# Opening stage of a two-layer trunk: two products instead of three, weights ahead of the modulation units, 256 channels at a time

## The chip, the cores and the metric

The kernel runs on one core of a Trainium2 chip. The metric is the device time of one execution in microseconds (us). The engines of the core are TensorE (PE, with PEld for its weight loads), VectorE (DVE), ScalarE (ACT), GpSimd (POOL) and SyncE (SP), whose queue issues nearly all transfers here. Sixteen DMA engines move the data.

## The reference

A decoder trunk of two layers over 256 tokens and 2048 channels, in float32. What matters here is how layer 0 begins:

```python
shift, scale, gate = jnp.split(jax.nn.silu(c) @ ada_w + ada_b, 3, axis=-1)
h = x * (1.0 + scale) + shift
proj = h @ w_in                      # q, k, v, o, gates of mLSTM | r, k, v, low ranks of RWKV-7
ya = _mlstm(...)                     # chunked matrix memory, 8 heads of 128
yb = _rwkv7(...)                     # state of 64 x 64 for 16 heads
y = jnp.concatenate([ya, yb], -1) @ w_out
x = layer_norm(ALPHA * x + (1.0 + gate) * y, ...)
```

After it follow a SwiGLU sub-layer and a second layer (retention and gated DeltaNet, then SwiGLU), each with a modulation of its own. The change leaves them as they are.

## The kernel before

**Products.** A product is h (256 tokens x 2048 channels) times 512 columns of weights. Float32 operands are split into two parts of type fp32r: ScalarE rounds a weight tile to `hi` (line 693), VectorE subtracts to get `lo` (line 694), and three matmuls per 128 channels and 128 tokens are summed in PSUM (lines 708 to 710: h's high part times `hi`, times `lo`, h's low part times `hi`). A *unit* is the part of a product over 512 channels (a quarter of the 2048): one weight tile of 128 x 2048 (1024 KB, from `w_ab`), two `hi` and two `lo` tiles of 128 x 1024, and 24 matmuls (2 halves x 2 token tiles x 2 blocks of 128 channels x 3). The weight tiles come in through a ring of three buffers, `raw`; the `hi` and `lo` tiles have three buffers each. A product has two banks of PSUM, out of a pool "g" of three; there are pools "m" of three and "c" of two beside it.

**Modulation (adaLN) units.** The vector silu(c) @ ada_w is 192 columns of 128 values. Each column is one unit: a weight tile of 128 x 2048 (1024 KB, `ada`) is multiplied on VectorE by `silu_c`, which holds silu(c) in all 128 partitions, and summed along the row (line 634, a SCALAR_TENSOR_TENSOR and a small read of the accumulator). After 8 units (4 shifts, 4 scales) lines 642 to 645 make bias and scale of 4 x 128 channels.

**Opening stage** (`setup`, `first_products`, `first_h`). It loads the constants (`cols`, `cons`, `crow` broadcast to 128 partitions, `rows`), applies Silu, and goes through the four quarters of the channels. For each quarter: 8 modulation units, then h for 512 channels (line 770 on ScalarE, 757 and 758 on VectorE), then a unit of each of four products: the low ranks (304 columns, `w_low`) and blocks 0, 1 and 2 of RWKV's columns. All eight PSUM banks are taken by these four products. Even modulation units use the ring `raw`, odd ones a larger pool `a`; all the weights of the products use `raw`. So 32 modulation units of 1024 KB and 16 weight tiles go in.

**Behind it** (`mixer_ab`, `rwkv`). RWKV runs in four batches of four heads; each has a front part and a chain of small float32 matmuls and VectorE steps (an inverse among them). The other products of layer 0 (RWKV blocks 3 to 5, mLSTM blocks 6 to 9, then 10 to 13) come in program order behind the batches: two after batch 0, two after batch 1, three after batch 2, the last four in the second mLSTM group. Results wait in two tiles `zt`, or go to DRAM (`put_by`). After each unit of a product, `fill(rate)` adds modulation units at 48/44 per unit: 48 of them over the 44 units of the 11 products.

**Order.** At the end of the program a planner (`Plan`) lists all instructions and fixes an order for every engine: lower program order first among what is ready, with the splits of a product moved 2000 places ahead. An instruction that opens a tile must wait until the ring of that tile has a free buffer, in program order within the ring. On the chip each engine, and SP's queue, then runs in this fixed order.

Lines that the steps below name: 597 to 611 (constants), 630 and 671 (transfers of weights), 634 (modulation), 642 to 645 (bias and scale), 693 and 694 (split), 708 to 710 (matmuls), 757, 758 and 770 (h), 1074 and 1082 (results out of PSUM), 998 to 1031 and 1188 to 1264 (RWKV's chain), 1322 (mLSTM's convolution).

Of the kernel before, what the change touches and what calls it, by code (L numbers as in the profile page):

```python
# [21 lines left out]
P = 128  # L22
# [13 lines left out]
LEVELS = (16, 32, 64)  # L36
HEAD = ("qz", "aa", "ss")
# [488 lines left out]
class Trunk:  # L526
# [67 lines left out]
    def setup(self):  # L594
        nc, fix = self.nc, self.fix
        self.cols = fix.tile([P, NCOLS], F32, name="cols_sb")
        nc.sync.dma_start(self.cols[:], self.ins["cols"])
        self.cons = fix.tile([P, NCONS], F32, name="cons_sb")
        nc.sync.dma_start(self.cons[:], self.ins["cons"])
        self.ident = self.con("ident")  # L600
        self.sc = fix.tile([P, D], F32, name="silu_c")
        nc.sync.dma_start(self.sc[:], self.ins["crow"].to_broadcast([P, D]))
        nc.scalar.activation(self.sc[:], self.sc[:], AF.Silu)
        o = COLS["mu_r"][0]
        self.keep = fix.tile([P, 27], F32, name="one_less_mu")
# [5 lines left out]
        nc.sync.dma_start(self.rows[:], self.ins["rows"].to_broadcast([P, 32]))  # L611
# [12 lines left out]
    def ada_unit(self, u, deep):  # L624
# [10 lines left out]
        ob = COLS["adab"][0] + 48 * sub  # L635
        if i < 32:
# [7 lines left out]
            if sub == 0:  # L644
                v.tensor_copy(bi, sh)
            else:
                og, ol = COLS["lng"][0] + 16 * (sub - 1) + 4 * g, COLS["lnb"][0] + 16 * (sub - 1) + 4 * g
                v.tensor_tensor(bi, self.cols[:, ol:ol + 4], sc, ALU.mult)
                v.tensor_tensor(bi, bi, sh, ALU.add)
                v.tensor_tensor(sc, self.cols[:, og:og + 4], sc, ALU.mult)  # L650
# [18 lines left out]
    def raw(self, src):  # L669
        w = self.raw_p.tile([P, 2048], F32, tag="raw", name=self.name("raw"))  # L670
# [3 lines left out]
    def split(self, src, n, ahead=2000, homes="ss"):  # L674
# [3 lines left out]
        with self.tc.high_priority(offset=ahead):  # L678
            w = self.raw(src)
# [80 lines left out]
    def first_h(self, g):  # L760
        nc = self.nc
        act = self.h_p.tile([P, 2, 4, T], F32R, tag="h", name=self.name("h"))
        for k2 in range(2):
            h32 = self.t2([P, 2, T])
            x = self.t2([P, 2, T])
            o = (4 * g + 2 * k2) * T
            nc.sync.dma_start(x[:], self.ins["xt"][:, o:o + 2 * T].rearrange("p (k t) -> p k t", k=2))
            for j in range(2):
                k = 4 * g + 2 * k2 + j
                nc.scalar.activation(h32[:, j, :], x[:, j, :], AF.Identity, bias=self.ab[:, 0, 16 + k:17 + k], scale=self.ab[:, 0, k:k + 1])  # L770
            self.into(act, slice(0, T), h32[:], slice(2 * k2, 2 * k2 + 2))
        return act
# [319 lines left out]
    def rwkv_tiles(self, zt, block):  # L1092

        nc = self.nc
        if block == 5:
            src, zt = zt, self.own([P, NT, 512], "zt", 2)
            self.fetch(zt, src)
# [169 lines left out]
    def first_products(self):  # L1267

        w, low = self.ins["w_ab"], self.ins["w_low"]
        srcs = [[low[i] for i in range(KG)]] + [[w[4 * b + i] for i in range(KG)] for b in range(3)]  # L1270
        banks = [[self.bank(k) for k in kinds] for kinds in ("gg", "gm", "mm", "cc")]
        h = []
        for g in range(KG):
# [5 lines left out]
        return h, [banks[0], self.by_tokens(banks[1])] + [self.by_tokens(banks[2 + i], two[:, i]) for i in range(2)]  # L1279

    def rwkv(self, product, early, beside, after):
# [6 lines left out]
        made = 0  # L1288
        last = None
        for i in range(4):  # L1290
# [17 lines left out]
            if i == 0:  # L1308
                tokens += [self.by_tokens(product(3 + j)) for j in range(2)]
            elif i == 1:  # L1310
                tokens.append(self.put_by(product(5)))
            after(i)
# [372 lines left out]
    def mixer_ab(self, h, rate, early):  # L1685
# [7 lines left out]
        def spilled(i, out):  # L1693
# [3 lines left out]
            if i == 2:  # L1697
# [3 lines left out]
        def direct(i, out):  # L1701
            banks = product(10 + i)
# [9 lines left out]
        def after(i):  # L1712
            for _ in range((0, 1, 3, 0)[i]):
# [58 lines left out]
def body(tc, ins, out):  # L1772
    with ExitStack() as stack:
# [6 lines left out]
        side = k.mixer_ab(h, 48.0 / 44, early)  # L1780
# [28 lines left out]
```

## Time and profile before

| | us |
|---|---|
| median of 3 runs (2826.0 to 2829.94) | 2829.93 |
| the profiled execution | 2830.83 |
| its span, first to last instruction | 2829.1 |
| PE busy (95%) | 2684.7 |
| DVE busy (72%) | 2023.7 |
| ACT busy (45%) | 1260.0 |

The mean granted clock of TensorE was 0.977 of full speed. DMA moved 683.80 MB, 242 GB/s over the span. Matmuls are pipelined, so that neighbours overlap in their busy times; the pitch from start to start is what they cost. Where a row gives a granted clock, 1.00 is 2.4 GHz and 0.50 is 1.2 GHz; what lies between is a mean over both.

### The profile page before, as it was taken

To read this page: it belongs to the slowest core of one execution; us is meant where nothing else is said; L and a number is where in the kernel's file an instruction comes from. 1 tells how busy PE (TensorE), PEld (TensorE's weight loads), DVE (VectorE), ACT (ScalarE), POOL (GpSimd) and SP (SyncE) were. 2 spreads that over 40 slices of the span, in tenths; PEclk is the share of its full clock that TensorE was granted. 3 is DMA by queue.
4 is the path that set the end of the run, shared out by engine and by line. 5 is a ranking of instruction groups with operands and counts; after the bars stand their busy time and mean duration, and the time that the engine had idled before them with its cause. 6 is when DMAs were issued, how large, how long until landed. Compare 5 with 4: busy or idle time off the path is not lost.

```text
span 2829.1 us, 33250 instructions
## 1 busy us (share of the span) xinstructions
PE 2684.7 (95%) x12622; PEld 2204.3 (78%) x12622; DVE 2023.7 (72%) x3189; ACT 1260.0 (45%) x1670; POOL 72.0 (3%) x88
## 2 busy tenths in 40 slices
PE   3699999899999999999999999999999999999997
PEld 2577777687788787888778888888778888888886
DVE  7889777677867557767767898885876646557557
ACT  1364443537544444443346544344454444443442
POOL 0000000100000000000000111000000000000000
PEclk9899998799999999999999999999999999999999
DMA  9878565255568668877865776675656757666554
GB/s 401 328 268 300 182 233 213 76 194 206 206 233 324 252 237 320 323 273 289 307 254 191 260 281 213 234 256 197 223 208 250 261 189 262 226 213 239 190 191 164
DMA packets 110536, 683.80 MB, mean 242 GB/s; under 512 B 12516, under 2 KB 15784, under 8 KB 32168
## 3 DMA queue, kind: packets, MB, share of 16 engines
q1 hardware_dynamic: 108936, 679.05, 65.8%
q10 hardware_dynamic: 1440, 2.62, 0.2%
q8 instruction: 99, 1.62, 0.2%
q14 instruction: 61, 0.50, 0.0%
HBM read 670.58 MB, written 11.04 MB: 241 GB/s over the span
## 4 chain that ended last, share of the span: by engine, by line
PE 64%; DVE 9%; DMA 8%; ACT 2%; issue 1%; POOL 0%; DVEq 0%; ACTq 0%
PE g L709 19%; PE g L710 19%; PE g L708 19%; DMA raw<-gu 3%; DVE lo L694 3%; DMA raw<-ada 2%; DVE raw L634 2%; ACT hi L693 1%; PE m L1017 1%; PE m L1024 1%; DMA t<-x 1%; DMA raw<-w_cd 1%; PE m L952 1%; DMA raw<-dn 1%; PE m L1031 0%
## 5 line engine op out<-in xcount | busy, mean ns | idle before, releaser
L694 DVE TENSOR_TENSOR lo<-raw,hi 128x1024 fp32r<-128x1024 f32 (+3 forms) x826 | 994.6, 1211 | 594.5 <-ACT hi L693 591.2
L693 ACT ACTIVATE hi<-raw 128x1024 fp32r<-128x1024 f32 (+3 forms) x826 | 860.2, 1048 | 1217.1 <-PE g L710 855.0
L708 PE MATMUL g<-hi,h 128*128 128x512 f32 (+3 forms) x2304 | 904.7, 394 | 72.6 <-ACT hi L693 44.8
L709 PE MATMUL g<-lo,h 128*128 128x512 f32 (+3 forms) x2304 | 905.4, 393 | 12.1 <-DVE lo L694 11.9
L710 PE MATMUL g<-hi,h 128*128 128x512 f32 (+3 forms) x2304 | 901.3, 392 | 0.0
L708 PEld LDWEIGHTS g<-hi,h 128*128 128x128 f32 x2304 | 439.0, 191 | 165.0 <-ACT hi L693 47.5
L709 PEld LDWEIGHTS g<-lo,h 128*128 128x128 f32 x2304 | 439.5, 191 | 110.5 <-DVE lo L694 24.4
L710 PEld LDWEIGHTS g<-hi,h 128*128 128x128 f32 x2304 | 439.0, 191 | 85.1 <-issue 1.3
L634 DVE SCALAR_TENSOR_TENSOR raw<-raw,silu_c 128x2048 f32<-128x2048 f32 x176 | 403.1, 2291 | 43.0 <-DMA raw<-ada 41.5
L708 PE MATMUL g<-hi,a 128*128 128x512 f32 x920 | 362.0, 394 | 7.2 <-DVE t L849 5.3
L709 PE MATMUL g<-lo,a 128*128 128x512 f32 x920 | 361.4, 393 | 1.8 <-DVE lo L694 1.8
L710 PE MATMUL g<-hi,a 128*128 128x512 f32 x920 | 360.0, 392 | 0.0
L708 PEld LDWEIGHTS g<-hi,a 128*128 128x128 f32 x920 | 173.8, 189 | 45.0 <-DVE t L849 6.0
L709 PEld LDWEIGHTS g<-lo,a 128*128 128x128 f32 x920 | 174.1, 189 | 38.0 <-DVE lo L694 3.0
L710 PEld LDWEIGHTS g<-hi,a 128*128 128x128 f32 x920 | 174.0, 189 | 36.1
L1328 DVE SCALAR_TENSOR_TENSOR f<-c,cols_sb,f 128x253 f32<-128x253 f32 (+2 forms) x120 | 56.3, 477 | 3.4 <-ACT f L1325 2.7
L1523 POOL TENSOR_SCALAR s<-cons_sb,log_alpha 128x128 f32<-128x128 f32 x16 | 19.4, 1228 | 1030.5 <-DVE log_alpha L1467 881.8
L634 DVE SCALAR_TENSOR_TENSOR a<-a,silu_c 128x2048 f32<-128x2048 f32 x16 | 36.2, 2288 | 1.3 <-DMA a<-ada 1.0
L891 ACT ACTIVATE t<-m,affine 128x128 f32<-128x128 f32 x96 | 34.9, 467 | 0.1
L1188 PE MATMUL m<-y 64*128 64x256 f32 x128 | 31.1, 454 | 2.2 <-DVE a L1191 1.9
L955 ACT ACTIVATE a<-m 128x512 fp32r<-128x512 f32 x44 | 25.9, 591 | 13.6 <-PE m L952 12.5
L1032 ACT ACTIVATE y<-m 128x512 f32<-128x512 f32 x24 | 13.9, 596 | 37.7 <-PE m L1031 37.3
(430 smaller groups left out, 2119.1 us busy)
## 6 DMA issues: line engine op xcount, KB each, us to landing
raw<-ada SPq DMA_DIRECT2D x176, 1024.0 KB, 4.9
raw<-gu SPq DMA_DIRECT2D x176, 1024.0 KB, 5.1
raw<-dn SPq DMA_DIRECT2D x88, 1024.0 KB, 4.8
raw<-w_cd SPq DMA_DIRECT2D x60, 1024.0 KB, 5.1
raw<-w_ab SPq DMA_DIRECT2D x56, 1024.0 KB, 5.8
a<-ada SPq DMA_DIRECT2D x16, 1024.0 KB, 16.8
raw<-o_ab SPq DMA_DIRECT2D x16, 1024.0 KB, 4.8
raw<-o_cd SPq DMA_DIRECT2D x16, 1024.0 KB, 4.8
```

The costliest lines, as they stand in the source:

```text
L634: v.scalar_tensor_tensor(w[:], w[:], 1.0, self.sc[:], ALU.mult, ALU.mult, accum_out=m[:, i:i + 1])
L693: nc.scalar.activation(hi[:, :2 * n], ws, AF.Copy)
L694: nc.vector.tensor_tensor(lo[:, :2 * n], ws, hi[:, :2 * n], ALU.subtract)
L708: mm(o, ah, wh, start=start and k == 0, stop=False)
L709: mm(o, ah, wl, start=False, stop=False)
L710: mm(o, al, wh, start=False, stop=stop and k == 3)
L891: nc.scalar.activation(h32[:, j, :], b[:, P * j:P * j + P], AF.Identity, bias=self.ab[:, sub + 1, 16 + k:17 + k], scale=self.ab[:, sub + 1 ...
L952: nc.tensor.transpose(b[:, P * k:P * k + P], gs[:, t, P * k:P * k + P], self.ident)
L1017: nc.tensor.matmul(x[:, 64 * j:64 * j + 64], mt[:, hs.start + j, :], dv[:, hs.start + j, :, 0, :], start=True, stop=True)
L1024: nc.tensor.matmul(x[:, 256 + 64 * j:320 + 64 * j], dt[:, hs.start + j, :], y[:, j, :], start=True, stop=True)
L1188: mm(b[:, T * x:T * x + T], bk[r, c, x, t, :], ar[r, c, t].rearrange("p x s -> p (x s)"), start=True, stop=True)
L1328: v.scalar_tensor_tensor(o[:, d:T], b[:, T * j:T * j + T - d], self.col(wname, 4 * (tile0 + i + j) + 3 - d), o[:, d:T], ALU.mult, ALU.add)
```

## The change

1. The opening stage accumulates the low ranks and two blocks (`WHOLE = 2`), not three. Block 2 becomes a usual product behind RWKV's batch 0. It has six PSUM banks.
2. In each quarter the x tiles and the three weight tiles are asked for ahead of the quarter's modulation units (in quarter 0 behind the first four). The weights land in the pool `y`, which is idle in this stage, not in `raw`. Their first halves are split into the usual `hi` and `lo` buffers, their second halves into the pools `q4` and `zt`, idle in this stage too.
3. The modulation units of layer 0's first 32 columns come in the order 0, 1, 4, 5, 2, 3, 6, 7 of each eight, so that after four units bias and scale of 256 channels are there, and h and the matmuls go by 256 channels.
4. `crow` comes in as one row of 8 KB. Four matmuls with a row of ones spread it to 128 partitions, and ScalarE applies Silu out of PSUM. `cons` and `rows` stand at the end of the stage in program order.
5. The other products are dealt out anew: blocks 2 and 6 after batch 0, blocks 3, 4 and 7 after batch 1, blocks 5, 8 and 9 after batch 2 (`TOK`, `SP`). Block 5 stays in `zt`; its trip to DRAM is gone. The modulation units come at 48/32 per unit of a product, so all 48 of them go with the first eight products and none with the last four.

`BEGUN = 0`: the two new functions for products that are begun in the opening stage are not called.

```diff
+BEGUN = 0
+SP = (1, 1, 2, 0)
+TOK = (1, 2, 1, 0)
+FIRST = ("sq", "sz", "sq")
+WHOLE = 2
...
         self.cons = fix.tile([P, NCONS], F32, name="cons_sb")
-        nc.sync.dma_start(self.cons[:], self.ins["cons"])
         self.ident = self.con("ident")
+        row = self.y8([P, D])
+        nc.sync.dma_start(row[0:1, :], self.ins["crow"])
+        ones = self.t1([P, P])
+        nc.vector.memset(ones[0:1, :], 1.0)
         self.sc = fix.tile([P, D], F32, name="silu_c")
-        nc.sync.dma_start(self.sc[:], self.ins["crow"].to_broadcast([P, D]))
-        nc.scalar.activation(self.sc[:], self.sc[:], AF.Silu)
+        for i, kind in enumerate("ccgg"):
+            s = slice(512 * i, 512 * i + 512)
+            b = self.bank(kind)
+            nc.tensor.matmul(b[:], ones[0:1, :], row[0:1, s], start=True, stop=True)
+            nc.scalar.activation(self.sc[:, s], b[:], AF.Silu)
...
-                self.ada_unit(self.ada_next, deep)
+                u = self.ada_next
+                self.ada_unit(u if u >= 32 else u - u % 8 + (0, 1, 4, 5, 2, 3, 6, 7)[u % 8], deep)
...
+        if sub == 0 and i < 32:
+            if i % 8 in (5, 7):
+                k = 4 * (i // 8) + i % 8 - 5
+                j = i // 8 * 8 + i % 8 - 5
+                v.tensor_tensor(self.ab[:, 0, 16 + k:18 + k], m[:, j:j + 2], self.cols[:, ob + j:ob + j + 2], ALU.add)
+                v.scalar_tensor_tensor(self.ab[:, 0, k:k + 2], m[:, j + 4:j + 6], 1.0, self.cols[:, ob + j + 4:ob + j + 6], ALU.add, ALU.add)
+            return
...
+    def first_x(self, g, i):
+        x = self.t2([P, 2, T])
+        o = (4 * g + 2 * i) * T
+        self.nc.sync.dma_start(x[:], self.ins["xt"][:, o:o + 2 * T].rearrange("p (k t) -> p k t", k=2))
+        return x
+
+    def first_h(self, act, g, i, x):
+        for j in range(2):
+            k = 4 * g + 2 * i + j
+            self.nc.scalar.activation(x[:, j, :], x[:, j, :], AF.Identity, bias=self.ab[:, 0, 16 + k:17 + k], scale=self.ab[:, 0, k:k + 1])
+        self.into(act, slice(0, T), x[:], slice(2 * i, 2 * i + 2))
...
-        banks = [[self.bank(k) for k in kinds] for kinds in ("gg", "gm", "mm", "cc")]
+        banks = [[self.bank(k) for k in kinds] for kinds in ("gg", "gm", "mm")[:1 + WHOLE]]
         h = []
         for g in range(KG):
-            self.ada(8, True)
-            h.append(self.first_h(g))
-            for p in range(4):
-                self.unit(srcs[p][g], 304 if p == 0 else 512, h[g], banks[p], g == 0, g == KG - 1, 0)
-        two = self.a8([P, 2, NT, 512])
+            h.append(self.h_p.tile([P, 2, 4, T], F32R, tag="h", name=self.name("h")))
+            xs = [self.first_x(g, i) for i in range(2)]
+            if g == 0:
+                self.ada(4, True)
+            widths = [304] + [512] * WHOLE
+            parts = [self.split(src[g], n, 0, home, self.y8) for src, n, home in zip(srcs, widths, FIRST)]
+            for i in range(2):
+                if g or i:
+                    self.ada(4, True)
+                self.first_h(h[g], g, i, xs[i])
+                for p, n in enumerate(widths):
+                    for t in range(NT):
+                        self.part(parts[p][i], i, n, h[g], t, banks[p][t], g == 0, g == KG - 1)
...
+        self.nc.sync.dma_start(self.cons[:], self.ins["cons"])
+        self.nc.sync.dma_start(self.rows[:], self.ins["rows"].to_broadcast([P, 32]))
+        return h, [banks[0]] + [self.by_tokens(b) for b in banks[1:]]
...
+            for _ in range(TOK[i]):
+                tokens.append(self.by_tokens(product(len(tokens))))
+            for _ in range(SP[i]):
                 cols.append(self.put_by(product(6 + len(cols))))
...
-        side = k.mixer_ab(h, 48.0 / 44, early)
+        side = k.mixer_ab(h, 48.0 / 32, early)
```

## Rows read from the trace of the kernel before

**Rows 1.** Windows, opening stage: length, busy us (instructions) per engine, clock, DMA share, GB/s.

```profile
core 0: us, PE busy (x) PEld busy (x) DVE busy (x) ACT busy (x) POOL busy (x), PEclk, DMA share, GB/s
20.00:60.00 40.00, 17.12 (x55) 12.97 (x56) 35.19 (x38) 8.03 (x11) 0.00 (x0) 0.96 1.02 427
60.00:80.00 20.00, 9.64 (x43) 7.66 (x41) 19.36 (x19) 1.61 (x2) 0.10 (x1) 0.82 0.97 399
80.00:161.40 81.40, 65.86 (x288) 54.96 (x289) 60.29 (x79) 35.79 (x47) 0.00 (x0) 0.90 0.82 301
```

**Rows 2.** Timeline, PE, opening stage: start, duration, line, out<-in, shape, idle before, releaser.

```profile
126.21 0.39 PE L708 MATMUL m<-hi,h 128*128 128x512 f32 x1
...
132.79 0.39 PE L710 MATMUL c<-hi,h 128*128 128x512 f32 x1
137.89 0.62 PE L708 MATMUL g<-hi,h 128*128 128x304 f32 x1 [4.72 <-DVE h L757]
...
140.84 0.42 PE L710 MATMUL g<-hi,h 128*128 128x304 f32 x1
...
161.25 0.39 PE L710 MATMUL c<-hi,h 128*128 128x512 f32 x1
```

**Rows 3.** Timeline, ScalarE, the first split of the second quarter.

```profile
82.30 1.31 ACT L693 ACTIVATE hi<-raw 128x608 fp32r<-128x608 f32 x2 [19.72 <-DMA raw<-w_low]
```

**Rows 4.** Timeline, SP's queue and VectorE, the start.

```profile
1.70 0.42 SPq L602 DMA_DIRECT2D silu_c<-crow  x1
...
12.22 2.29 DVE L634 SCALAR_TENSOR_TENSOR raw<-raw,silu_c 128x2048 f32<-128x2048 f32 x1 [8.28 <-DMA raw<-ada]
```

**Rows 5.** Timeline, PE, a float32 matmul over 256 columns.

```profile
169.06 1.03 PE L1120 MATMUL c<-q,low_ranks 65*128 65x256 f32 x4
```

**Rows 6.** Timeline, VectorE: modulation units, splits and h.

```profile
67.28 2.28 DVE L634 SCALAR_TENSOR_TENSOR a<-a,silu_c 128x2048 f32<-128x2048 f32 x1
...
73.91 2.28 DVE L634 SCALAR_TENSOR_TENSOR a<-a,silu_c 128x2048 f32<-128x2048 f32 x1
...
83.35 1.49 DVE L694 TENSOR_TENSOR lo<-raw,hi 128x608 fp32r<-128x608 f32 x2
84.76 0.42 DVE L757 CAST h<-t 128x512 fp32r<-128x512 f32 x1
85.21 0.69 DVE L758 TENSOR_TENSOR h<-t,h 128x512 fp32r<-128x512 f32 x1
...
120.22 2.36 DVE L694 TENSOR_TENSOR lo<-raw,hi 128x1024 fp32r<-128x1024 f32 x2 [2.57 <-ACT hi L693]
```

**Rows 7.** Windows, behind the opening stage, columns as in rows 1.

```profile
161.40:460.00 298.60, 289.54 (x1503) 229.98 (x1501) 248.20 (x567) 155.08 (x265) 14.35 (x16) 0.99 0.68 247
460.00:545.00 85.00, 71.83 (x333) 57.84 (x332) 48.11 (x157) 29.18 (x63) 7.38 (x11) 0.66 0.22 82
545.00:640.00 95.00, 92.86 (x537) 78.41 (x535) 75.02 (x182) 43.78 (x76) 5.32 (x10) 1.00 0.55 200
```

**Rows 8.** Windows, line 634 alone (two instructions per unit): VectorE busy, clock, DMA.

```profile
161.40:460.00 298.60, 75.97 (x66) 0.99 0.68 247
...
545.00:640.00 95.00, 20.78 (x19) 1.00 0.55 200
```

**Rows 9.** Timeline, SP's queue: batch 2's first transfer; product weights around a pause.

```profile
329.22 0.33 SPq L1115 DMA_DIRECT2D q<-lw  x1
...
477.86 0.33 SPq L671 DMA_DIRECT2D raw<-w_ab  x1
...
549.29 0.34 SPq L671 DMA_DIRECT2D raw<-w_ab  x1
```

**Rows 10.** Chain of work that ended last, VectorE ahead of an inverse; PE behind it.

```profile
466.45 1.16 DVE lo L694
...
468.49 2.15 DVE raw L634
471.57 0.70 DVE y L1002
```

More of the change, by code (lines that the diff above doesn't have):

```diff
@@ L666, in gate_rows, with raw, split @@
         return gate
-    def raw(self, src):
-        w = self.raw_p.tile([P, 2048], F32, tag="raw", name=self.name("raw"))
+    def raw(self, src, room=None):
+        w = room([P, 2048]) if room else self.raw_p.tile([P, 2048], F32, tag="raw", name=self.name("raw"))
         self.nc.sync.dma_start(w[:, :src.shape[-1]], src)
         return w
-    def split(self, src, n, ahead=2000, homes="ss"):
+    def split(self, src, n, ahead=2000, homes="ss", room=None):
         nc = self.nc
         with self.tc.high_priority(offset=ahead):
-            w = self.raw(src)
+            w = self.raw(src, room)
             parts = []
@@ new lines, in first_products @@
+            for i in range(2):
[5 more added lines that the diff above has]
+                        self.part(parts[p][i], i, n, h[g], t, banks[p][t], g == 0, g == KG - 1)
+            if g == 1:
+                for b in range(6, 6 + BEGUN):
+                    self.begun.append((b, self.first_rows(b, h)))
+        self.nc.sync.dma_start(self.cons[:], self.ins["cons"])
@@ new lines, in first_products, with first_rows @@
+        self.nc.sync.dma_start(self.rows[:], self.ins["rows"].to_broadcast([P, 32]))
+        return h, [banks[0]] + [self.by_tokens(b) for b in banks[1:]]
+    def first_rows(self, b, h):
+        i = b - 6
+        if i < 4:
+            if i % 2 == 0:
+                self.pair = self.a8([P, 2, NT, 512]) if i == 0 else self.y8([P, 2, NT, 512])
+            z = self.pair[:, i % 2]
+        else:
+            z = self.q4([P, NT, 512])[:]
+        banks = [self.bank("c") for _ in range(NT)]
+        for g in range(2):
+            self.unit(self.ins["w_ab"][4 * b + g], 512, h[g], banks, g == 0, g == 1, 0)
+        for t in range(NT):
+            self.nc.scalar.activation(z[:, t, :], banks[t][:], AF.Copy)
+        return z
@@ new lines, in other_rows @@
+    def other_rows(self, h, rate):
+        b, z = self.begun.pop(0)
+        banks = [self.bank("g") for _ in range(NT)]
+        for g in (2, 3):
+            self.unit(self.ins["w_ab"][4 * b + g], 512, h[g], banks, g == 2, g == 3)
+            self.fill(rate)
+        dst = self.dram.tile([T, 512], F32, name=self.name("by"))
+        for t in range(NT):
+            self.nc.vector.tensor_tensor(z[:, t, :], banks[t][:], z[:, t, :], ALU.add)
+            self.nc.scalar.dma_start(dst[P * t:P * t + P, :], z[:, t, :])
+        return dst
@@ L1307, in rwkv @@
             finish(side)
[L1308 to L1312, printed above, removed]
+            after(i, tokens)
     def conv(self, zt, outs, wname, tile0):
@@ L1701, in direct @@
         def direct(i, out):
+            if len(cols) > 4 + i:
+                return spilled(4 + i, out)
             banks = product(10 + i)
@@ L1710, in beside, with after @@
             return self.mlstm_group(0, spilled) if i == 3 else iter(())
-        def after(i):
-            for _ in range((0, 1, 3, 0)[i]):
+        def after(i, tokens):
+            if i == 0:
+                for _ in range(BEGUN):
+                    cols.append(self.other_rows(h, rate))
+            for _ in range(TOK[i]):
+                tokens.append(self.by_tokens(product(len(tokens))))
+            for _ in range(SP[i]):
                 cols.append(self.put_by(product(6 + len(cols))))
```

35 lines of the change are left out of this document (8 added, 27 removed).

## The prediction

> **What bounds the kernel now.** I read the page's slices first, then the windows of the opening stage, then the timelines that set its pace, then the windows behind it.
>
> TensorE is busy nearly everywhere except in the first 160 us and in one stretch near 460 to 545 us. The opening stage ends when its last matmul starts at 161.25 us [rows 2]. Its work is small against that. The pitch of a matmul over 512 columns at full clock is (132.79 - 126.21) / 29 = 0.227 us [rows 2]; over 304 columns I scale that by the columns to 0.135. Four low-rank units are 4 x 24 x 0.135 = 13.0 us and twelve full units 12 x 24 x 0.227 = 65.4 us, 78.4 us together. So 83 of 161 us are waiting or half clock.
>
> What it waits for changes inside the stage. From 20 to 60 us the DMA engines are full at 427 GB/s, and VectorE is busy for 35.19 of 40 us; from 60 to 80 us VectorE is busy for 19.36 of 20 us [rows 1]. From 80 us on neither is full: DMA 0.82, VectorE 60.29 of 81.40 us [rows 1]. There weights and modulation units take turns in one ring of three buffers. ScalarE, for one, sat idle for 19.72 us for the second quarter's low-rank tile [rows 3], whose transfer had no free buffer until modulation units were done.
>
> Behind the stage TensorE is the bound up to 460 us: 289.54 of 298.60 us busy at clock 0.99 [rows 7]. Then the products run out. No weights are asked for between 477.86 and 549.29 us [rows 9], and from 460 to 545 us PE is idle for 85 - 71.83 = 13.2 us and runs at a mean clock of 0.66 [rows 7]. At that clock about 71.83 x 0.34 = 24.4 us of its busy time is lost. Together that is a hole of 37.6 us.
>
> **The change, part by part.**
>
> *The opening stage, by bytes.* Modulation 32 x 1.049 MB, low ranks 4 x 0.62, blocks 8 x 1.049, x 2.1, `cols` 0.3 and `cons` 0.6 make 47.4 MB. At 427 GB/s [rows 1] that is 111 us. The first modulation unit started at 12.22 us [rows 4], behind 3.0 MB (7.1 us at that rate), so the stream begins at about 5 us and ends at 116 us.
>
> *By VectorE.* A modulation unit has a pitch of (73.91 - 67.28) / 3 = 2.21 us; a pair of `lo` tiles 1.49 us (304 columns) or 2.36 us (512, pitch 1.14 each); h of 256 channels 85.21 + 0.69 - 84.76 = 1.1 us [rows 6]. So 32 x 2.21 + 4 x 1.5 + 16 x 1.14 + 8 x 1.1 + about 3 for bias and scale = 107 us. It starts earlier: the broadcast `crow` (1 MB, issued at 1.70 us) [rows 4] and `cons` are no longer in front, only `cols`, one row and 0.5 MB of x. Against that Silu now waits for four float32 matmuls. The nearest row has four over 256 columns in 1.03 us at full clock [rows 5]; over 512 columns and at half clock that is up to 4 us, and it ends near the time when the first unit lands. I take 9 us for the first unit. SP's queue passes nothing in the way: 8 KB, and `cons` is issued when the weight buffers are full; it is first needed by the transposes behind the stage, long after.
>
> So both limits lie near 116 us, and neither fully hides the other. VectorE reached 19.36 / 20 = 97% and 35.19 / 40 = 88% where DMA was full [rows 1]; 107 us at these shares are 110 and 122, so it ends at 119 or 131. I take the middle, 125.
>
> *The tail.* The last half quarter's matmuls can start only after the last h: 12 over 304 columns and 24 over 512. Behind 4.72 us of idle time the 304s ran at half clock, eleven pitches in 140.84 - 137.89 = 2.95 us [rows 2]. After that 24 x 0.227 = 5.4 us. That is 8.4 us, from a little before VectorE's end. The stage ends at 125 + 6 = 131 us, with bounds of 126 and 140.
>
> *What moves.* Block 2's four units, 4 x 24 x 0.227 = 21.8 us of PE at full clock, now run behind the stage, where PE is the bound. The opening alone is worth 161.4 - 131 - 21.8 = 8.6 us (bounds 13.6 and -0.4). The break-even is an end at 139.6 us.
>
> *The hole.* RWKV's chain and the products start together 30 us earlier, and there is one more product to fill with. Seven products, 152.6 us of PE, lasted from 161 us to the last transfer near 480 [rows 9]: 0.48 us of product per us. One more lasts 21.8 / 0.48 = 45 us. The chain gets on in that time, and the hole at 460 shrinks. Its bounds: nothing, or the product's 21.8 us. I take 11.
>
> *The modulation rate.* Instead of 48/44 per unit over 28 units (30.5 columns) the first eight products carry 48: 17.5 x 2.21 = 38.7 us more of VectorE, and 8 x 1.14 = 9.1 us for block 2's `lo`. VectorE has 298.60 - 248.20 + 85 - 48.11 = 87 us to spare there [rows 7], in the wrong places partly: where products run at their pace it is nearly full, and the chain's small steps queue behind units of 2.2 us, as at 468.49 us ahead of the step at 471.57 [rows 10]. Bounds: nothing, or 36 us (47.8 / 0.83, VectorE's share now, less the product's 21.8). I take 4, because the pause has the room.
>
> *Behind 545 us.* The last four products lose their 20.78 us of line 634 [rows 8], but PE is busy for 92.86 of 95 us there [rows 7]: 0 to 2.1, I take 1.
>
> *Waits that are new.* Block 5 now waits for a `zt` buffer, that of block 3, which batch 2's front frees; blocks 8 and 9 queue behind it in pool "g". Batch 2's first transfer is issued 168 us behind the stage's end [rows 9], and the sixth product ends, at 0.48 us per us, 6 x 21.8 / 0.48 = 270 us behind it. So this costs nothing. If batch 2 slipped by 100 us, it would be a pause like the one at 478 us [rows 9]. Block 2 itself is needed by batch 1 only. Dropping block 5's trip to DRAM, the smaller h code and the second-half buffers are nothing: ScalarE is busy for 155 of 299 us [rows 7], and the buffers' former users come after the stage.
>
> **The sum**, against the profiled 2830.83 us: 8.6 + 11 - 4 + 1 = 16.6, so 2814.2. The median of the runs was 0.9 us lower than the profiled run, so 2813.3, rounded to 2813.
>
> A rule speaks against the opening's price. The rows show 427 GB/s over 40 us and 399 over the next 20 [rows 1]. The Trainium skill (DMA: Bandwidth & Descriptors, Specifications) gives a limit of about 358 GB/s for a core's share of HBM, under a fabric ceiling of 435. Where buffers are free, the trace stands with the higher figure, but no run here shows it for over 60 us; what the lower one would do is rival 4.
>
> **Rivals.** *1: the chain decides.* If RWKV's chain sets the time up to 545 us, all of it moves up by the 30 us of the opening, and the extra product vanishes in the hole. For it: the hole of 37.6 us is larger than the product. Against it: PE is full for 300 us ahead. Gain 8.6 + 21.8 + 1 = 31.4, less some waiting: 2800.
>
> *2: the opening doesn't get as short as it is meant to.* The split of 256 channels gives VectorE eight hand-overs to ScalarE and back. If it is kept at 88% [rows 1], the stage ends at 140 us, and the moved product takes all of it back: -0.4 with 0 to 6 from the hole, 2827.
>
> *3: VectorE becomes the bound behind the opening (slower).* It adds 47.8 us to a VectorE that is at 83% [rows 7]. If the product stretch runs at its pace, PE idles, and its clock falls as it did at 460. It decides from the point where the added wait passes what opening and hole give, 8.6 + 11 = 20 us. At its bound of 36 us: 16 us slower, and with half of the hole's clock loss kept out of it, 2840.
>
> *4: HBM holds the long stream.* With 40 us at 427 GB/s it is unlikely [rows 1]. If the whole stage ran at the mean rate of 301 to 399 of its later windows [rows 1], 350, the stream would last 135 us, end at 140, and the stage at 155: 15 us slower, 2840 with some of the hole filled. The skill's 358 GB/s, by itself, would give 132 us of stream, an end at 152 and about 2836.
>
> **How the numbers follow.** Forecast (gains of 6 to 25 us) 0.53, rival 1 0.19, rival 2 0.13, rival 3 0.11, rival 4 0.04. About 0.2%, 5.7 us, is what a measurement of this kernel can tell. Faster is forecast and rival 1, 0.72; the same is rival 2, 0.13; slower is rivals 3 and 4, 0.15. The range reaches from rival 1 with a stage end at 126 us, 2795, to 2834, on the way to the slower cases: opening at its worst and half of VectorE's bound.
>
> **What would show it.** The opening right: last w_ab matmul of the stage near 131 us, DMA share over 0.95 and VectorE over 90% from 20 to 115 us, no wait of ScalarE for weights. Wrong: a stage end past 139.6 us. The hole right: weights asked for until about 500 us, and PE's idle time and low clock up to the start of block 10 well under 37 us. Rival 1: that hole gone. Rival 3: VectorE over 93% with PE idle between 130 and 460 us, and a clock under 0.9 there. Behind 545 us little should change. What would make all of it wrong: an order by the planner that puts transfers of one quarter behind buffers of the next, which the trace of before can't show.

## The result, and the profile after

The changed kernel takes 2793.08 us (median, 2789.58 to 2795.68) against 2829.64 us (2826.0 to 2829.94): ratio 0.9873, 95% interval 0.9856 to 0.989. That is 36.6 us less, where 16.6 were forecast; the time lies 2 us below the predicted range. The profiled execution took 2789.58 us, span 2787.6 us, mean granted clock 0.984. It is 3.5 us quicker than its median, and that of before was 1.2 us slower than its own, so the two profiled executions differ by 4.7 us more than the medians do; their spans differ by 41.5 us.

Four places divide the span: the stage's end (first transposes behind the last product matmul), the end of the pause in `w_ab` transfers, the first transfer of feed-forward weights (`gu`), and the end. In the changed kernel, timeline of PE, then of SP's queue:

```profile
138.74 0.39 PE L725 MATMUL m<-q,h 128*128 128x512 f32 x1
138.96 0.27 PE L1074 MATMUL m<-cons_sb,q 128*64 128x128 f32 x1
```

```profile
451.48 47.48 SPq L686 DMA_DIRECT2D raw<-w_ab  x4
519.39 4.78 SPq L686 DMA_DIRECT2D raw<-w_ab  x2
...
711.67 0.33 SPq L686 DMA_DIRECT2D raw<-gu  x1
```

The stage ended at 161.4 us [rows 2], now at 138.9. The pause ended at 549.29 us [rows 9], now at 519.39, and it begins at 499 (451.48 + 47.48), not at 477.86. The first `gu` was asked for at 744.72 us, now at 711.67.

The windows of the opening, which answer [rows 1] (columns as there):

```profile
20.00:60.00 40.00, 21.38 (x72) 16.91 (x72) 34.67 (x41) 11.28 (x16) 0.00 (x0) 0.80 1.00 418
60.00:80.00 20.00, 10.91 (x43) 9.51 (x44) 19.24 (x23) 4.53 (x6) 0.32 (x1) 0.76 1.01 423
80.00:100.00 20.00, 7.23 (x31) 5.88 (x30) 18.73 (x18) 5.23 (x7) 0.00 (x0) 0.76 1.01 425
100.00:138.90 38.90, 32.86 (x144) 27.97 (x145) 34.30 (x49) 15.93 (x22) 0.00 (x0) 0.88 0.83 324
```

The windows behind it, which answer [rows 7], and then the modulation line (645, once 634) alone, which answers [rows 8]:

```profile
138.90:460.00 321.10, 307.84 (x1568) 242.80 (x1567) 283.56 (x632) 160.60 (x272) 13.00 (x16) 0.98 0.75 278
460.00:545.00 85.00, 81.47 (x477) 67.50 (x475) 60.20 (x183) 47.35 (x90) 8.51 (x11) 0.98 0.29 100
545.00:640.00 95.00, 94.05 (x545) 78.45 (x545) 53.09 (x139) 49.48 (x84) 10.43 (x17) 1.00 0.25 91
```

```profile
139.00:460.00 321.00, 104.86 (x92) 0.98 0.75 278
460.00:545.00 85.00, 0.00 (x0) 0.98 0.29 100
545.00:640.00 95.00, 0.00 (x0) 1.00 0.25 91
```

From 460 to 545 us PE was busy for 71.83 us at 0.66 [rows 7], now for 81.47 at 0.98. The hole is nearly gone. The 20.78 us of modulation behind 545 us [rows 8] are gone as well.

**A ledger of lost TensorE time.** For a window, loss is its length less PE's busy time multiplied by the granted clock: idling and low clock in one number. Before, then after, from the stage's end to the first `gu`:

```profile
161.40:300.00 138.60, 133.52 (x691) 106.61 (x689) 122.47 (x240) 76.89 (x121) 6.89 (x5) 1.00 0.76 280
300.00:460.00 160.00, 156.02 (x814) 123.38 (x814) 125.73 (x328) 78.19 (x144) 7.46 (x11) 0.99 0.61 219
460.00:549.30 89.30, 76.13 (x352) 61.36 (x351) 52.04 (x168) 33.47 (x71) 7.38 (x11) 0.68 0.25 90
549.30:744.70 195.40, 190.76 (x973) 156.39 (x972) 151.44 (x328) 104.30 (x157) 12.31 (x20) 0.98 0.54 194
```

```profile
138.90:300.00 161.10, 153.78 (x774) 122.39 (x772) 143.99 (x269) 80.83 (x130) 5.17 (x6) 0.97 0.80 299
300.00:460.00 160.00, 154.06 (x796) 120.41 (x795) 139.57 (x363) 79.78 (x142) 7.83 (x10) 1.00 0.69 256
460.00:519.40 59.40, 55.87 (x357) 46.32 (x356) 37.19 (x121) 28.15 (x63) 8.51 (x11) 0.97 0.16 54
519.40:711.70 192.30, 191.35 (x999) 158.45 (x998) 135.20 (x319) 108.84 (x165) 11.66 (x20) 1.00 0.41 148
```

The third row before: 89.3 - 76.13 x 0.68 = 37.5 us lost; after: 59.4 - 55.87 x 0.97 = 5.2. The clock is given to 0.01, so one entry is good to 1 or 2 us. What is left when the losses are taken from the distance is work: 583.3 - 56.6 = 526.7 us before, 572.8 - 24.0 = 548.8 after. The 22.1 us between them are the moved product (21.8). So the forecast's sum can be set beside the two profiled executions, term by term:

| term, us gained | forecast | measured |
|---|---|---|
| end of the opening | 30.4 | 161.4 - 138.9 = 22.5 |
| product moved behind it | -21.8 | 526.7 - 548.8 = -22.1 |
| loss up to 460 us (rate) | -4 | 10.6 - 17.8 = -7.2 |
| loss in the hole | 11 | 37.5 - 5.2 = 32.3 |
| loss from there to `gu` | 1 | 8.5 - 1.0 = 7.5 |
| behind the first `gu` | 0 | 2084.4 - 2075.9 = 8.5 |
| sum | 16.6 | 41.5 |

### The profile page after: what moved, and what is told of

Read it like the earlier page. It is cut to its first block, busy times and chain, and to the rows that moved or that the text cites. A ratio compares the mean times of both kernels' runs of the same rounds, so it can differ in the third digit from the quotient of the medians.

```text
span 2787.6 us, 33284 instructions
## 1 busy us (share of the span) xinstructions
PE 2666.1 (96%) x12630; PEld 2188.2 (78%) x12630; DVE 2023.3 (73%) x3194; ACT 1260.5 (45%) x1673; POOL 71.3 (3%) x88
## 4 chain that ended last, share of the span: by engine, by line
PE 74%; DVE 11%; DMA 10%; ACT 2%; issue 2%; SPq 0%; POOL 0%; DVEq 0%; ACTq 0%
PE g L724 21%; PE g L723 21%; PE g L725 21%; DVE lo L709 3%; DVE raw L645 3%; DMA raw<-ada 3%; DMA raw<-gu 3%; ACT hi L708 2%; PE m L1038 1%; DMA raw<-w_ab 1%; PE m L1031 1%; PE m L966 1%; DVE a L645 1%; DMA y<-w_ab 1%; DMA rows_sb<-rows 1%
## 5 line engine op out<-in xcount | busy, mean ns | idle before, releaser
L709 DVE TENSOR_TENSOR lo<-raw,hi 128x1024 fp32r<-128x1024 f32 (+2 forms) x802 | 970.4, 1217 | 580.2 <-ACT hi L708 576.5
L708 ACT ACTIVATE hi<-raw 128x1024 fp32r<-128x1024 f32 (+2 forms) x802 | 838.8, 1052 | 1132.1 <-PE g L725 881.4
L723 PE MATMUL g<-hi,h 128*128 128x512 f32 (+2 forms) x2312 | 905.8, 393 | 42.9 <-DVE h L772 35.9
L724 PE MATMUL g<-lo,h 128*128 128x512 f32 (+2 forms) x2312 | 907.5, 393 | 10.9 <-DVE lo L709 10.4
L725 PE MATMUL g<-hi,h 128*128 128x512 f32 (+2 forms) x2312 | 904.5, 391 | 0.0
L724 PEld LDWEIGHTS g<-lo,h 128*128 128x128 f32 x2312 | 439.2, 190 | 108.8 <-DVE lo L709 21.8
L708 ACT ACTIVATE hi<-y 128x1024 fp32r<-128x1024 f32 (+1 forms) x12 | 11.3, 942 | 47.9 <-DMA y<-w_ab 30.0
L969 ACT ACTIVATE a<-m 128x512 fp32r<-128x512 f32 x44 | 25.8, 591 | 12.6 <-PE m L966 11.5
L1052 POOL TENSOR_SCALAR_AFFINE_SELECT a<-a 128x512 f32<-128x512 f32 (+1 forms) x20 | 22.9, 1152 | 312.4 <-ACT a L1201 286.0
## 6 DMA issues: line engine op xcount, KB each, us to landing
a<-ada SPq DMA_DIRECT2D x16, 1024.0 KB, 17.3
```

What stands on the lines that cost most here:

```text
L708: nc.scalar.activation(hi[:, :2 * n], ws, AF.Copy)
L709: nc.vector.tensor_tensor(lo[:, :2 * n], ws, hi[:, :2 * n], ALU.subtract)
L723: mm(o, ah, wh, start=start and k == 0, stop=False)
L724: mm(o, ah, wl, start=False, stop=False)
L725: mm(o, al, wh, start=False, stop=stop and k == 3)
L969: nc.scalar.activation(act[:, 0, :, ts], bv, AF.Copy)
```

## The experiments

In the diffs, `-` is the kernel that is named first. S is the stage's end, P the end of the pause, G the first `gu`. The ledger, in us, one profiled execution of each kernel:

| kernel | S | S to G | lost up to 460 | in the hole | from P to G | median us |
|---|---|---|---|---|---|---|
| before | 161.4 | 583.3 | 10.6 | 37.5 | 8.5 | 2829.64 |
| e2, before + product | 166.3 | 569.4 | 4.4 | 10.4 | 8.1 | 2826.93 |
| e5, before, rate 48/32 | 165.3 | 573.5 | 28.2 | 20.5 | 1.0 | 2826.5 |
| e3, two products alone | 144.8 | 584.6 | 32.6 | 2.3 | 0.9 | 2807.1 |
| after | 138.9 | 572.8 | 17.8 | 5.2 | 1.0 | 2793.08 |
| e1, after, rate 48/44 | 140.5 | 581.4 | 6.7 | 26.3 | 0.0 | 2812.65 |
| e14, ring, rate 48/36 | 134.3 | 583.1 | 17.7 | 20.3 | 0.0 | 2807.28 |
| e8, ring, rate 48/28 | 133.8 | 580.4 | 28.1 | 0.2 | 1.1 | 2799.94 |
| e13, after, rate 48/24 | 139.2 | 606.2 | 47.9 | 0.7 | 7.1 | 2824.32 |
| e12, rate 48/44 braked | 143.0 | 596.5 | 32.3 | 5.7 | 13.1 | 2823.66 |
| e7, weights in the ring | 154.7 | 573.1 | 17.3 | 7.2 | 1.0 | 2816.03 |
| e6, constants first | 141.2 | 572.1 | 19.0 | 5.3 | 0.9 | 2798.33 |
| e4, three in the ring | 133.7 | 574.3 | 23.7 | 0.4 | 0.9 | 2790.77 |
| e9, after, other order | 138.2 | 573.6 | 16.9 | 6.3 | 2.0 | 2810.86 |

The places scatter from one execution to the next. The opening of the kernel before ended at 161.4, 165.3, 166.3 and, in e10 below, 165.8 us, that of the changed kernel at 138.2 to 140.7 us where neither opening nor brake was altered, so the opening's gain is 21 to 28 us. The distance from S to G was 572.8, 574.5 and 570.9 us in three profiles of the changed kernel and 574.3, 570.0 and 569.8 in three of e4, so a difference under 5 us there tells nothing. One program's times scatter, too: those of the kernel before went from 2813.83 to 2840.93 us on one chip. So medians of different chips are compared only where they differ by more than 5 us, and steps by the places in the profile.

**What is the moved product worth?** The kernel before computes block 5 a second time behind batch 0 and puts the result, which nothing reads, to DRAM:

```
 def after(i):
+    if i == 0:
+        self.put_by(self.product([w[4 * 5 + k] for k in range(KG)], 512, h))
```

> The kernel before, with one product more: block 5 is computed a second time behind batch 0 and its result written to DRAM and left there (96 matmuls, 21.8 us of TensorE at full clock, 4 MB of weights, no modulation columns with it). Nothing else changes. Theory 1 (the chain decides; the hole of 37.6 us at 460 to 545 us takes the product in): 2830 to 2836 us. Rival (TensorE decides, and the hole moves along behind the added work): 2830 + 22 = 2852. Halfway: 2841.

Ratio 0.9997 (0.9976 to 1.0017): a whole product, 21.8 us of TensorE, costs nothing. Its hole:

```profile
460.00:540.70 80.70, 74.83 (x424) 59.76 (x423) 64.62 (x177) 41.27 (x77) 7.38 (x11) 0.94 0.50 177
```

The loss is 10.4 us in place of 37.5: busier and at 0.94 in place of 0.68. More than the product's own time comes back, since the work also keeps the clock up. The idea that TensorE's work decides up to the feed-forward part falls.

**What is the rate worth, alone and with the product?** First the old rate in the changed kernel, then the new rate in the kernel before:

```
-side = k.mixer_ab(h, 48.0 / 32, early)
+side = k.mixer_ab(h, 48.0 / 44, early)
```

> The changed kernel, with the modulation columns at 48/44 per unit of a product again, so that they reach into the last four products. Theory 1 (RWKV's chain sets the time from the end of the opening stage to the pause in the product weights, and the rate pays behind the pause, where the changed kernel was 8 us shorter): that stretch goes back from 192 towards 200 us, the one ahead of it stays within 4 us of 381; the time is 2797 to 2802 us. Rival (the rate is worth nothing; the 8 us come from the earlier start): 2793, within 3.

> The kernel before with the modulation rate 48/32 and nothing else. The changed kernel lost about 20 us when that rate was put back. Theory 'the rate is worth something by itself': units that run behind the pause in the kernel before (about 20 us of VectorE) delay the second half of the mixer, and the kernel before gains 8 to 20 us from the rate alone: 2808 to 2820. Theory 'the rate pays only together with the moved product' (VectorE's room in the product stretch comes from the longer stretch): 2824 to 2832. Prediction's own step: a cost of 4 less 1, about 2831.

e1 takes 2812.65 us, ratio 0.9943 (0.9919 to 0.9966), well outside both expectations, and its stretches went the other way: 395.0 us from S to P and 186.4 from P to G. e5 takes 2826.5, 0.9999 (0.9984 to 1.0015), inside the range of "only together with the moved product". The hole of e1, then hole and last stretch of e5:

```profile
460.00:535.50 75.50, 60.05 (x338) 46.76 (x337) 51.85 (x179) 35.37 (x74) 7.32 (x11) 0.82 0.23 78
```

```profile
460.00:546.40 86.40, 74.90 (x412) 59.43 (x412) 58.40 (x187) 39.45 (x79) 7.25 (x11) 0.88 0.33 128
546.40:738.80 192.40, 191.45 (x999) 158.49 (x999) 135.63 (x323) 104.79 (x160) 11.57 (x20) 1.00 0.41 148
```

In e5 the rate takes 17 us out of the hole and puts 17.6 into the stretch before it (28.2 against 10.6); what it wins up to G, 9.8 us, is the loss behind the pause (7.5) and rounding. In the changed kernel it takes 21.1 us from the hole for 11.1 before it: 8.6 us from S to G. So up to the feed-forward part the rate is worth some 9 us either way, though in e5 the total does not show it.

**The two products alone**, with the old loads, 512 channels at a time and old constants:

```
-srcs = [[low[i] for i in range(KG)]] + [[w[4 * b + i] for i in range(KG)] for b in range(3)]
+srcs = [[low[i] for i in range(KG)]] + [[w[4 * b + i] for i in range(KG)] for b in range(2)]
...
-side = k.mixer_ab(h, 48.0 / 44, early)
+side = k.mixer_ab(h, 48.0 / 32, early)
```

> The kernel before with two things of the change alone: the opening stage accumulates two blocks, and the products and modulation columns are dealt out as in the changed kernel (blocks 2 and 6, then 3, 4 and 7, then 5, 8 and 9; 48/32 per unit). Constants, ring of weights, quarters of 512 channels and order of the columns stay as before. Theory 1: the stage ends 8 to 12 us earlier, near 150 us (4 MB and 9 us of VectorE less), all of it passes through, and 8 us more come behind the pause: 2808 to 2815 us. Rival A (TensorE decides, the moved product costs its 21.8 us): 2830 to 2842. Rival B (loading ahead, 256 channels and constants are worth nothing): 2793.

2807.1 us, 0.994 (0.9916 to 0.9964). The stage ends at 144.8 us, earlier than the 150 expected: dropping one product gives 16.6 of the opening's 22.5 us by itself, the new loads some 6 more. The hole is closed here too (2.3 us), but 32.6 us are lost before it.

**Do the new loads matter, and does the opening's end pass through?** The quarter's weights go through the ring of three again:

```
-parts = [self.split(src[g], n, 0, home, self.y8) for src, n, home in zip(srcs, widths, FIRST)]
+parts = [self.split(src[g], n, 0, home) for src, n, home in zip(srcs, widths, FIRST)]
```

> The changed kernel, but the opening's quarter weights go through the ring of three again and not through the idle tiles ahead of their modulation units. 28 loads in place of 16 then share the three buffers. The stage should end 5 to 12 us later, at 144 to 151 us against 138.7 to 140.6. Theory 'the opening's end passes through': the time is 5 to 12 us above the changed kernel's, 2798 to 2805. Theory 'half of it is lost in the hole behind': 2796 to 2799.

```profile
20.00:100.00 80.00, 35.97 (x132) 29.62 (x133) 66.80 (x74) 17.64 (x23) 0.10 (x1) 0.70 0.91 367
```

DMA moves 367 GB/s and not 421 over these 80 us, and the stage ends at 154.7 us, later than expected and later than with the old loads of e3. S to G is 573.1 us: the whole delay arrives at the feed-forward part, G at 727.8 against 711.7. The total is 2816.03 us, 23 above the changed kernel's; the 7 us beyond the stage's delay arise behind G.

Then constants first, with the broadcast transfer and one activation, as before:

```
+nc.sync.dma_start(self.cons[:], self.ins["cons"])
...
-row = self.y8([P, D])
...
+nc.sync.dma_start(self.sc[:], self.ins["crow"].to_broadcast([P, D]))
+nc.scalar.activation(self.sc[:], self.sc[:], AF.Silu)
```

> The changed kernel with the old start: constants loaded first, the condition row broadcast by a transfer of 1 MB, one activation over it, no float32 matmuls. Theory 'VectorE's first unit sets the opening': the first unit starts at 13 to 15 us in place of 11.4, the stage ends 2 to 4 us later than 138.9, the time is 2 to 4 us above the changed kernel's. Theory 'the ring of three paces the stage's end, whatever its start': stage end within 1 us of 138.9, time within 1 us.

The first unit starts at 13.04 us and not at 11.40 to 11.52, and the stage ends at 141.2 against 140.7 for the unaltered kernel beside it: the start does not set the end, as the second theory had it. The median, 2798.33, is 5.3 us above that kernel's, more than either theory allowed, but G stood 1.8 us earlier, and the ratio, 0.9897 (0.9875 to 0.9919), overlaps that of the unaltered kernel on the same chip, 0.9882 (0.9858 to 0.9906).

> The changed kernel, unaltered, as the anchor for the three kernels beside it: about 2793 us, ratio to the kernel before near 0.987. If it comes out several us away from that, differences of that size between kernels taken on different chips prove nothing.

Then three of eight opening units in the ring, and not four:

```
-if deep and i % 2:
+if deep and i % 8 not in (0, 4, 6):
```

> The changed kernel, with column 2 of each eight of the opening stage in the pool of five buffers as well, so that five of eight columns use that pool and three the ring of three (before four and four). In the changed kernel's last quarter all the columns left are in the ring of three, and both halves of h come late. Theory 2 (that ring sets the end of the stage): it ends at 130 to 135 us instead of 139, and the time is 2785 to 2790. Rival (VectorE and DMA are full anyway): 2793, within 3.

> The changed kernel with three of eight opening modulation units in the ring of three and five in the other buffers, now beside the changed kernel itself. Theory 'the opening's end passes through to the end of the program': its stage ends 5 us earlier (133.7 against 138.9 us), so the time is 4 to 6 us below the changed kernel's. Theory 'a part of it is eaten by the products that follow, since TensorE is the bound there': 0 to 3 us below.

> The version with three of eight opening units in the ring, once more beside the changed kernel. Its stage ended 5 us earlier in two profiles, and its times stood 2 to 5 us below the changed kernel's. If the opening passes through: 3 to 6 us below. If not: within 2.

> The changed kernel, unaltered, beside the two ring versions: 2791 to 2795, ratio to the kernel before 0.987 to 0.988.

The stage ended at 133.7, 135.4 and 134.7 us, the changed kernel's at 138.9, 140.7 and 140.5; G stood at 708.0, 705.4 and 704.5 against 711.7, 715.1 and 711.4. So the ring did pace the tail: moving one unit in eight brought its end forward by 5.2 to 5.8 us, and G by 3.7 to 9.7. The totals do not settle it: 2790.77, then 2788.17 beside 2793.07, then 2794.52 beside 2794.05. On the last chip the profiled run took 2087.3 us from G to the end, where the same program had taken 2078.5 and 2076.2. A version that beats the changed kernel is not shown.

**Where is the rate's best, and why?** Thirteen VectorE products as long as a unit (results not used) are added to the old rate, spread over the first 32 product units. Then the rates 48/24, and 48/28 and 48/36 with the ring version:

```
+if rate > 1.0 and getattr(self, "brakes", 0) < 32:
...
+    self.brake_credit = getattr(self, "brake_credit", 0.0) + 48.0 / 32 - 48.0 / 44
+    while self.brake_credit >= 0.999:
...
+            self.nc.vector.scalar_tensor_tensor(t[:], self.sc[:, s], 1.0, self.sc[:, s], ALU.mult, ALU.mult)
```

> The changed kernel with the old modulation rate 48/44, and beside it 13 further VectorE products of the same length (four pieces of 512 columns each, results not used) spread over the first 32 product units, so that VectorE has as much to do between the products as at rate 48/32, while twelve modulation units still run behind the pause. From the end of the stage to the first weights of the feed-forward part it took 570 to 574 us at 48/32 and 581 at 48/44. Theory 'the faster rate slows the products, so RWKV's chain gets TensorE earlier and products are left to fill the hole': 570 to 577 here, and time 2790 to 2805. Theory 'the faster rate pays because no units are left behind the pause': 581 or more, 2812 or more.

> The changed kernel with the modulation rate 48/24: all 48 units in the first six products. Theory 'slowing the products moves work into the hole': the hole is already nearly gone at 48/32 (5 us lost between 460 and 519 us), so nothing more is to be had: stage end to feed-forward 570 to 577 us. Rival 3 of the prediction, 'VectorE becomes the bound', from this point on: PE idles before 300 us, 580 to 590 us, time 2800 to 2810.

> The version with three of eight opening units in the ring (2788 to 2791) with the rate 48/28 in place of 48/32. If the hole is gone at 48/32 already: 2785 to 2793. If the order behind is drawn worse: up to 2805, with all of the difference behind the first weights of the feed-forward part.

> The version with three of eight opening units in the ring, with the rate 48/36. What TensorE loses by idling and by a low clock from the stage's end to the feed-forward part was 33 us at 48/44, 24 at 48/32, 29 at 48/28 (with this ring) and 56 at 48/24. If that is one valley with its floor between 44 and 28, 48/36 loses 22 to 28 us and stands within 4 us of the ring version: 2786 to 2794. If the floor is sharp at 32, the loss is 29 or more: 2795 or more.

One row each: e12 from 300 us, e13 from the stage's end, e14 in the hole.

```profile
300.00:460.00 160.00, 143.60 (x704) 114.69 (x704) 137.09 (x342) 68.04 (x119) 6.44 (x8) 0.91 0.54 195
```

```profile
139.20:300.00 160.80, 141.30 (x655) 110.08 (x654) 143.21 (x270) 69.96 (x115) 4.04 (x5) 0.89 0.79 298
```

```profile
460.00:528.20 68.20, 58.37 (x335) 46.12 (x335) 41.69 (x141) 31.47 (x66) 7.39 (x11) 0.82 0.18 64
```

At 48/24, 35.0 us are lost before 300 us: `hi` waits for 26.9 us there for `w_ab` transfers, and PE 10.5 us for `hi`. That is a form of rival 3's price; a part of it is paid at 48/28, where 28.1 us are lost up to 460 us, against 19.0 to 23.7 in the three profiles of e4, the same ring at 48/32. At 48/36 it is 20.3 us of hole, although a single unit of modulation, 2.17 us, is left in it and none behind it. So "units left behind the pause" does not explain the rate; and e12, 2823.66 us, refutes "slowing the products is enough", in the form in which the planner placed the brake: the brake empties the hole (5.7 us) and opens another at 300 to 460 us (29.3). What the runs show is loss before 460 us at the fast rates and loss in the hole at the slow ones, with the best of the five rates at 48/32. The floor is sharp, as e14's second expectation had it: 48/36 loses as much before 460 us (17.7) as 48/32 and still keeps its hole. Why is open.

**Is the rest the order?** The planner holds an engine back for a more urgent operation for 250 ns; with 350, the order of the same instructions differs from some 400 us on:

```
-plan = Plan(tc, tc.nc, 250)
+plan = Plan(tc, tc.nc, 350)
```

> The changed kernel with another order of the same work: the planner's time for which an engine is held back for a more urgent operation is 350 and not 250 ns. The order is the same up to some 400 us and differs behind it. Theory 'the gain behind the opening is the work that was moved': within 3 us of the changed kernel, 2790 to 2796. Theory 'orders drawn anew are worth 5 to 10 us by themselves, and part of the gain is such a draw': 2796 or more, or 2787 or less.

> The kernel before with the same other order (350 in place of 250 ns) and nothing else. Theory 'the gain is the work that was moved': 2826 to 2832. Theory 'orders drawn anew are worth 5 to 10 us': outside that.

> The changed kernel with the old modulation rate 48/44, in that other order. With the first order the old rate cost 19.5 us, of which the trace showed only 8.6 us up to the first weights of the feed-forward part; the rest was scattered behind it, where the rate changes no work. Theory 'the rate itself costs what it costs up to there, the rest was the order': 2798 to 2806. Theory 'the rate costs all of it': 2809 to 2816.

2810.86, 2850.08 and 2825.24 us: 17.8, 20.4 and 12.6 more than with 250, where 5 to 10 were expected of a new order; e11 lies above both of its ranges. e9 reaches G at 711.8 us, as the changed kernel does (711.7). From there on the same instructions took 2097.2 us and not 2075.9. The first feed-forward part of the changed kernel, then that of e9, from the first `gu` to the first `w_cd`:

```profile
711.70:1456.70 745.00, 733.84 (x3265) 599.70 (x3264) 532.77 (x573) 320.47 (x356) 0.00 (x0) 1.00 0.76 280
```

```profile
711.80:1471.90 760.10, 740.82 (x3275) 605.04 (x3274) 533.62 (x573) 321.62 (x357) 0.00 (x0) 0.99 0.75 275
```

That is 15 us more; in two further profiles of the changed kernel this part took 745.9 and 749.2 us, so 11 to 15 us are order alone. e11 also keeps the rate's cost up to G with that order: 586.2 us from S to G against e9's 573.6.

## Why the prediction was right or wrong

**The direction was right; the step that failed is the hole, and with it the modulation rate, which was taken for a cost alone.** The hole was priced at 11 us, half of the moved product; it gave 32.3. e1 divides that: with the moved product and the old rate the loss in the hole falls from 37.5 to 26.3 us, 11.2, as much as was forecast, and from e1 to the changed kernel the rate takes out the other 21.1. From S to G the forecast had -21.8 + 11 for the product and -4 + 1 for the rate, -13.8 us together. Measured were 583.3 - 581.4 = 1.9 for the product, nothing within the scatter, and 581.4 - 572.8 = 8.6 for the rate, 10.5 together.

The prediction let one product last 45 us at 0.48 us per us, but counted seven products before the pause where nine had been loaded, and priced the work that fits, not the clock. The row that gives 71.83 us at 0.66 [rows 7] already said that 24.4 us of the 37.6 were clock; work that fills the idle time gets that back too. e2 shows it: a product that brings no modulation units with it takes 27 us from the hole and costs nothing.

Nor had the products run out. SP's queue runs in a fixed order, and ahead of the next weights stood four transfers (`q<-by`, inputs of mLSTM) that waited for a matmul at the end of an RWKV batch. Before, then after, that matmul (timeline of PE), the transfers (timeline of SP's queue) and the queue's wait for it (total us, times, longest):

```profile
534.42 1.22 PE L1263 MATMUL c<-low_ranks,q 32*128 32x256 f32 x2
535.66 2.42 SPq L1090 DMA_DIRECT2D q<-by  x4
SPq L1090 <- PE c L1263: 57.5, 1, 57.5
```

```profile
511.13 0.69 PE L1274 MATMUL c<-low_ranks,q 32*128 32x256 f32 x2
511.86 2.18 SPq L1104 DMA_DIRECT2D q<-by  x4
SPq L1104 <- PE c L1274: 12.8, 1, 12.8
```

The queue stood at them for 57.5 us before, 50.2 in e5, 40.1 in e1, 21.6 in e2 and 12.8 in the changed kernel (holes of 37.5, 20.5, 26.3, 10.4 and 5.2). The matmul came 374 us behind the stage's end before and 373 after, so between these two the chain moved up with the opening. In other runs it came 362 (e2) to 395 us (e13) behind it; what sets that is open, and no run moves these transfers.

This is rival 1's mechanism, "the extra product vanishes in the hole": with the measured opening its sum is 22.5 + 1 = 23.5, and e1, the change without its rate, moved G by 22.8. It had 0.19, and it left out what the rate gave on top.

**The opening's end** was 138.9 us, not 131; the bounds 126 to 140 held it, the break-even at 139.6 was just met, so that by the forecast's own sum the opening alone was worth 0.7 us and not 8.6. The stream behaved as forecast: 418 to 425 GB/s to 100 us, VectorE 72.64 of 80 us (91%). ScalarE did wait for weights, 42.7 us in all, against the sign given. Rival 4, the mean of 350, is refuted. The Trainium skill's limit of 358 GB/s (DMA: Bandwidth & Descriptors, Specifications) did not hold here either: 421 GB/s over 80 us. The Trainium skill's HBM Reference (Specifications) adds that a core streaming alone reaches about 425, and the trace agrees with that. What was mis-sized is the end: VectorE's last h came at 127.58 + 0.69 = 128.27 us, where the forecast had 125, and the tail behind it took 10.6 us, not 6. VectorE's timeline (three of six units, the last h), SP's queue and PE:

```profile
101.20 2.28 DVE L645 SCALAR_TENSOR_TENSOR raw<-raw,silu_c 128x2048 f32<-128x2048 f32 x1
...
113.34 2.28 DVE L645 SCALAR_TENSOR_TENSOR raw<-raw,silu_c 128x2048 f32<-128x2048 f32 x1
...
122.86 2.29 DVE L645 SCALAR_TENSOR_TENSOR raw<-raw,silu_c 128x2048 f32<-128x2048 f32 x1
...
127.58 0.69 DVE L773 TENSOR_TENSOR h<-t,h 128x512 fp32r<-128x512 f32 x1
```

```profile
103.52 12.47 SPq L686 DMA_DIRECT2D raw<-ada  x3
```

```profile
123.00 0.62 PE L723 MATMUL g<-hi,h 128*128 128x304 f32 x1 [5.42 <-DVE h L772]
```

The last six units all lie in the ring of three, so that SP's queue hands them out one by one (three in 12.47 us), DMA falls to a share of 0.83, and both halves of the last quarter wait: 15.9 us of matmuls from 123.00 to 138.9, two halves and not one. e4 took 5.2 us off by moving one unit in eight; the prediction named such a planner's trap only as what it could not see.

**The first unit** started at 11.40 us, 9 forecast, behind the last Silu and no longer behind its data [rows 4]. It cost nothing (e6). The row for the float32 matmuls [rows 5] was misread: line 1120 is run twice, so its four instructions are two matmuls and not four.

```profile
11.40 2.29 DVE L645 SCALAR_TENSOR_TENSOR raw<-raw,silu_c 128x2048 f32<-128x2048 f32 x1 [7.30 <-ACT silu_c L614]
```

**The rate** was priced at a cost of 4, within 0 to 36. From e1 to the changed kernel 11.1 us are lost before 460 us, so sign and place of that cost were right; what the step left out is the 21.1 us won in the hole. Its 38.7 us of added VectorE work follow from the same count of seven products; only 20.78 us of units were left behind 545 us to be moved [rows 8]. That the products, held back, are then there for the hole is argued; e12, which held them back by other means, did not gain by it. Rival 3 did not come, but its bound was not idle: 48/24 loses 35 us before 300 us.

**Behind the pause**, 1 forecast, bound 2.1, 7.5 measured. The bound looked at 545 to 640 us only [rows 7] and left out the stretch up to the first `gu`, in which most of it was lost. e5 shows the same gain with the rate alone (1.0 us lost). But e1 loses 0.0 there with 13.77 us of modulation units behind the pause, so units left there are not the reason, and it stays open.

**The new waits** cost nothing, as forecast: e1, which has them at the old rate, loses 6.7 us before 460 us, the kernel before 10.6.

**Behind the first `gu`** nothing was forecast. 8.5 us were gained between the profiled runs; the same program scatters there by up to 11 us (e4), and the other order took 10.6 to 21.3 us more (e9 to e11). So this part is not tied to any edit. It is also why the totals of e1 and e7 are longer than their places say: G stood 10.2 and 16.1 us later than in the changed kernel, the medians are 19.6 and 23.0 us longer.

## What to carry to other kernels

Price a hole in TensorE's work by idle time plus clock loss together, and ask what fills it: work moved from a stage that is bound by transfers into such a hole can be free, and the prior question is whether the chain or the engine sets its end. A setting that spreads side work over such a stretch can have a sharp best value, and it needs a scan, since here the rates at both ends cost some 20 us and more. Ask also what the queue that asks for the weights stands behind: one transfer in a fixed order can hold all that follow. Where a planner draws the order, compare places in the trace up to which the order is the same, for a new order alone moved this kernel by 13 to 20 us.

## What the runs showed of the hardware

The four float32 matmuls that spread one row over 128 partitions took longer than the nearest row suggested (timeline of PE, start):

```profile
3.58 3.75 PE L613 MATMUL c<-y,s 1*128 1x512 f32 x4 [3.58 <-DMA y<-crow]
7.12 3.62 PE L613 MATMUL g<-y,s 1*128 1x512 f32 x4
```

They show as eight instructions, some 0.9 us each, where 1.03 us for four over 256 columns [rows 5] would give 0.5. The window from 3 to 11 us gives a clock of 1.00, so by that row the clock is not the reason, which stays open:

```profile
3.00:11.00 8.00, 7.16 (x8) 2.50 (x8) 0.33 (x3) 2.02 (x4) 0.00 (x0) 1.00 0.92 342
```

The DMA rate, not shown before for over 60 us, lasted: 418 to 425 GB/s for 80 us on end. Over the 38.9 us behind, in which SP's queue hands out the ring's three buffers one by one, it was 324.
